# One 256-column broadcast product for the MLP norm factors in place of two of 128 columns, with both diagonals written by one VectorE operation

## Chip, cores and metric

The kernel runs on one core of a Trainium2 chip. The metric is the device time of one execution in microseconds (us), lower is better. TensorE (PE) does the matrix products, VectorE (DVE), ScalarE (ACT) and GpSimd (POOL) the elementwise work, and SyncE (SP) issues the transfers of the weights from HBM. PEld stands for PE's loading of the stationary operand.

## What is computed

The reference is a decoder trunk of two layers, A and B, on 256 tokens of width 1024 in float32. Each layer is an attention part followed by an MLP with a squared ReLU behind an RMS norm. The change touches only the norm of the two MLPs:

```python
def _rmsnorm(x, g):
    xf = x.astype(jnp.float32)
    y = xf * lax.rsqrt(jnp.mean(xf * xf, axis=-1, keepdims=True) + EPS)
    return (y * g.astype(jnp.float32)).astype(x.dtype)

def _sq_relu_mlp(h, w_up, w_down):
    u = jax.nn.relu(h @ w_up)
    return (u * u) @ w_down
...
x = x + _sq_relu_mlp(_rmsnorm(x, a_norm_mlp[i]), a_w_up[i], a_w_down[i])
```

The factor rsqrt(mean + EPS) is one number for each token. The kernel multiplies x by the gains first, runs the up projection on that, and applies the factor of each token to the product, together with the ReLU. This is allowed since the factor is positive and common to a token's row.

## The kernel before

Activations lie transposed: 128 of the 1024 features on the partitions, the 256 tokens along the free dimension, eight such tiles (`xT`). Every float32 weight is split into a high part `wh`, written by ACT (line 336), and a low part `wl`, written by DVE (line 338). A product is then three matmuls: high by high, low by high, high by low.

**The up projection** (`mlp_up`, line 772) runs over 16 blocks, numbered 0 to 15 here. A block is two chunks of weights, each 128 of the 4096 hidden features, and fills one PSUM bank (128 x 512 float32, class `acc`, four banks) with 48 matmuls of 256 columns (line 819). DVE then empties the bank (line 788): ReLU and the multiplication by `rb`, the factors of the 256 tokens spread over all partitions. Block 0's line 788 is the first reader of `rb`.

**The factors.** ACT squares the tiles of x into buffers of the class `sq` (two of them), POOL adds them up (line 450), a small product with a matrix of ones sums over the partitions (line 458), and a chain of short DVE operations (lines 464 to 466) makes the factor `rstd`, 128 partitions x 2: partition p, column h is token 128h + p. **`bcast`** (line 470) turns that into `rb`: for each half h it writes a diagonal matrix, the identity times the factor column (line 475, buffers of the class `dg`), and multiplies it with the matrix of ones on PE (line 477), which leaves the 128 factors of that half in every partition of PSUM. DVE then copies the 256 columns to `rb` (line 479). This happens once in each layer, while PE is in the middle of the up projection.

**What sets the order.** Nothing runs in the order in which it is written. Each operation is given to a planner (`Plan.add`, lines 75 to 116) with its engine, an assumed duration in ns, and the buffers that it reads and writes. `Plan.order` (line 118) simulates the engines, starts whatever is ready with the lowest priority number, and hands out the buffers of a class as they come free, the lowest free number first. A buffer counts as free 200 ns (`LAT`) after the planned end of its last user. The program is then emitted in the planned order, and on the chip each engine works through its own queue in that order and waits on semaphores. So an assumed duration that changes can move instructions on any engine and can hand a buffer to another user. The planner's numbers for `bcast` before are 196 ns for each diagonal and 213 ns for each product.

Of the kernel before, what the change touches and what calls it, by code (L numbers as in the profile page):

```python
# [14 lines left out]
OP = mybir.AluOpType  # L15
AX = mybir.AxisListType

D, S, FF = 1024, 256, 4096
# [194 lines left out]
def t_dve(n, scalar=False):  # L213
    return 69 + 1.041 * n + (61 if scalar else 0)
# [11 lines left out]
def tile_hybrid(ctx: ExitStack, tc: tile.TileContext, xa, xb, memt, xnat, mnat, w0, wall, consts, fgain, out):  # L226
    nc = tc.nc
# [9 lines left out]
    P = Plan(caps, ("acc", "w", "wh", "wl", "v") + tuple(f"B{i}" for i in range(8)))  # L237
    uid = [0]

    def name(s):  # L240
        uid[0] += 1
        return f"{s}_{uid[0]}"

    def buf(cls, shape, dt=F32, pool=None):
        pool = pool or ring
        return Buf(cls, lambda slot: pool.tile(shape, dt, name=name(cls), tag=f"{cls}{slot}", bufs=1))

    def bank(cls):
        return buf(cls, [128, 512], F32, psum)
# [8 lines left out]
    def fixed(shape, nm, dt=F32):  # L258
        return const.tile(shape, dt, name=name(nm))
# [28 lines left out]
    ones = fixed([128, 128], "ones")  # L288
# [5 lines left out]
    ident = fixed([128, 128], "ident")  # L294
# [175 lines left out]
    def bcast(st):  # L470

        ps = bank("t")
        for h in range(2):
            dg = buf("dg", [128, 128])
            P.add(("dve", 196, lambda dg=dg, h=h: nc.vector.tensor_scalar_mul(dg.t, ident, st.r[:, h:h + 1])),
                  [st.key], [dg])
            P.add(("pe", 213, lambda dg=dg, h=h: nc.tensor.matmul(
                ps.t[:, h * 128:(h + 1) * 128], ones, dg.t, start=True, stop=True)), [dg], [ps])
        P.add(("dve", t_dve(S), lambda: nc.vector.tensor_copy(rb_t, ps.t[:, 0:S])), [ps], ["rb"])


# [290 lines left out]
    def mlp_up(st, sums=()):  # L772
# [5 lines left out]
        for b in range(16):  # L778
            u = buf("u", [128, 2, S])
            ps = bank("acc")  # L780
            for mi in range(2):
                wh, wl = chunk()
                up_chunk(ps, mi, wh, wl)
            if first:
                bcast(st)
                first = False
            k0 = 2 * b % 4
            P.add(("dve", t_dve(512, True), lambda u=u, ps=ps: nc.vector.scalar_tensor_tensor(  # L788
                u.t, ps.t.rearrange("p (a s) -> p a s", a=2), 0.0, rb_t[:, None, :].to_broadcast([128, 2, S]),
                op0=OP.max, op1=OP.mult)), [ps, "rb"], [u])  # L790
            P.add(("act", t_act(512), lambda u=u: nc.scalar.activation(u.t, u.t, AF.Square)), [u], [u])  # L791
            if b in sums:
                dst, keys = sums[b]

                def blocks(u=u, dst=dst):
                    a = [u.t[:, k, hf * 128:hf * 128 + 128] for hf in range(2) for k in range(2)]
                    s = [dst()[:, i * 128:i * 128 + 128] for i in range(4)]
                    nc.vector.tensor_add(s[0], a[2], a[3])
                    nc.vector.tensor_sub(s[1], s[0], a[0])
                    nc.vector.tensor_sub(s[2], a[0], a[2])  # L800
                    nc.vector.tensor_sub(s[3], a[1], s[1])
                P.add(("dve", 4 * t_dve(128) + 100, blocks), [u], keys, port=True)
            P.add(("act", t_act(512), lambda u=u, t=us[b // 2], k0=k0: nc.scalar.copy(t.t[:, k0:k0 + 2, 0], u.t)),
                  [u], [(us[b // 2], b)])
            P.add(("dve", t_dve(512), lambda u=u, t=us[b // 2], k0=k0: nc.vector.tensor_sub(
                t.t[:, k0:k0 + 2, 1], u.t, t.t[:, k0:k0 + 2, 0].bitcast(F32))), [u, (us[b // 2], b)],
                [(us[b // 2], b, 1)], port=True)
# [595 lines left out]
```

## Time and profile before

| | |
|---|---|
| median of 3 runs | 595.46 us (594.59 to 595.98) |
| the profiled execution | 598.83 us, of which the span from the first to the last instruction is 597.1 us |
| mean granted TensorE clock | 0.996 |
| busy: PEld / DVE / ACT / POOL | 517.7 / 485.2 / 390.1 / 56.1 us of the span |
| instructions on PE / DVE | 3794 / 869 |
| read from HBM | 106.72 MB, 181 GB/s over the span |

A share of busy time is a mean over the whole span. What a change in one place is worth is read from that place: which engine is working without a pause there, and which wait ends last. In a group's row the columns are the source line, the engine and operation, output<-input with the shape, the count, the busy time and the mean duration of one in ns, and after the second bar the idle time of the engine before these instructions and what ended it. In a timeline row they are the start, the time from the first start to the last end, the engine, the line, the names and the count. Durations include a tail that the next instruction overlaps, so the distance from start to start is shorter than the duration.

### The profile page before, as it was taken

Reading aid. Unit: us, or ns where it says so; the run is one execution under the profiler, and the core shown is the slowest. Engines: PE = TensorE matmul, PEld = TensorE weight load, DVE = VectorE, ACT = ScalarE, POOL = GpSimd, SP = SyncE. Lnnn points to the kernel's source line nnn. Section 1 sums busy time; section 2 is a strip of 40 time slices with the busy share of each in tenths; the row PEclk is TensorE's granted clock in tenths of the full one; section 3 lists DMA queues with packets and bytes.
Section 4 is the critical chain, followed back from the end, with each engine's and each line's share of the span. In section 5 each row is a group of like instructions: output and inputs, shape, how many; then the busy total and the mean of one; then the engine's idle time right before and its main releaser. Section 6 shows DMA issues by size and latency. Waiting matters only on the chain.

```text
span 597.1 us, 10365 instructions
## 1 busy us (share of the span) xinstructions
PE 586.0 (98%) x3794; PEld 517.7 (87%) x3794; DVE 485.2 (81%) x869; ACT 390.1 (65%) x749; POOL 56.1 (9%) x67
## 2 busy tenths in 40 slices
PE   8999999999999999999999999999999999999995
PEld 7777878999999988888888887889999999888884
DVE  6699886789877898988988688786886767998874
ACT  6788797666665575555786588776575565665632
POOL 0131020240000000000122131001300000000002
PEclk9999999999999999999999999999999999999998
DMA  8974715336656536567576633334565555356531
GB/s 302 343 259 137 257 65 167 118 122 228 207 182 209 181 111 224 193 209 247 173 232 233 211 125 124 106 93 159 183 205 199 188 178 177 141 177 245 180 104 71
DMA packets 30003, 108.45 MB, mean 182 GB/s; under 512 B 3328, under 2 KB 3328, under 8 KB 29696
## 3 DMA queue, kind: packets, MB, share of 16 engines
q1 hardware_dynamic: 29664, 107.26, 53.5%
q8 instruction: 30, 0.49, 0.3%
q10 hardware_dynamic: 288, 0.52, 0.2%
q14 instruction: 21, 0.17, 0.1%
HBM read 106.72 MB, written 1.05 MB: 181 GB/s over the span
## 4 chain that ended last, share of the span: by engine, by line
PE 88%; DMA 4%; DVE 4%; ACT 3%; issue 1%; SPq 0%; DVEq 0%; ACTq 0%
PE acc L819 30%; PE t L869 22%; PE acc L497 16%; PE acc L763 7%; PE acc L869 6%; DMA w<-wall 2%; PE t L584 2%; PE t L622 2%; PE t L679 1%; DVE wl L338 1%; DMA w<-memt 1%; ACT wh L336 1%; PE t L555 1%; DMA xT<-xa 1%; DVE xT L749 0%
## 5 line engine op out<-in xcount | busy, mean ns | idle before, releaser
L336 ACT CAST wh<-w 128x512 fp32r<-128x512 f32 (+1 forms) x232 | 182.4, 816 | 119.8 <-PE acc L819 44.5
L338 DVE TENSOR_TENSOR wl<-w,wh 128x512 fp32r<-128x512 f32 (+1 forms) x232 | 213.8, 943 | 32.6 <-ACT wh L336 32.0
L819 PE MATMUL acc<-xn,wh 128*128 128x256 f32 x1024 | 130.2, 279 | 1.1 <-DVE xn L354 1.1
L819 PEld LDWEIGHTS acc<-xn,wh 128*128 128x128 f32 x1024 | 123.4, 188 | 1.5 <-DVE xn L354 1.3
L869 PE MATMUL t<-wh,B 128*128 128x512 f32 (+1 forms) x368 | 111.9, 386 | 0.0
L497 PE MATMUL acc<-wh,xn 128*128 128x512 f32 x256 | 86.1, 404 | 0.9 <-ACT xn L352 0.9
L869 PEld LDWEIGHTS t<-wh,B 128*128 128x128 f32 x368 | 68.5, 188 | 13.8
L869 PE MATMUL t<-wl,B 128*128 128x512 f32 (+1 forms) x184 | 71.0, 386 | 0.0
L819 PE MATMUL acc<-xn,wl 128*128 128x256 f32 x512 | 70.1, 279 | 0.0
L819 PEld LDWEIGHTS acc<-xn,wl 128*128 128x128 f32 x512 | 64.0, 188 | 0.0
L497 PEld LDWEIGHTS acc<-wh,xn 128*128 128x128 f32 x256 | 48.9, 191 | 13.4 <-issue 1.4
L497 PE MATMUL acc<-wl,xn 128*128 128x512 f32 x128 | 50.9, 397 | 0.2 <-DVE wl L338 0.2
L763 PE MATMUL acc<-B,wh 128*128 128x256 f32 x256 | 50.8, 289 | 0.0
L450 POOL TENSOR_TENSOR sqa<-sqa,sq 128x256 f32<-128x256 f32 x21 | 20.3, 966 | 235.4 <-ACT sq L449 234.4
L788 DVE SCALAR_TENSOR_TENSOR u<-acc,rb 128x512 f32<-128x512 f32 x32 | 21.9, 690 | 24.6 <-PE acc L819 24.5
L763 PEld LDWEIGHTS acc<-B,wh 128*128 128x128 f32 x256 | 41.1, 191 | 0.6 <-issue 0.5
L869 PEld LDWEIGHTS t<-wl,B 128*128 128x128 f32 x184 | 34.6, 188 | 7.0
L763 PE MATMUL acc<-B,wl 128*128 128x256 f32 x128 | 36.1, 282 | 0.0
L531 POOL TENSOR_TENSOR ropet<-ropes,consts 128x256 f32<-128x256 f32 (+1 forms) x28 | 25.8, 940 | 105.1 <-ACT ropes L520 77.0
L892 ACT CAST wh<-wsum 128x1024 fp32r<-128x1024 f32 x24 | 25.3, 1052 | 8.6 <-PE acc L819 3.2
L791 ACT ACTIVATE u<-u 128x512 f32<-128x512 f32 x32 | 20.1, 632 | 16.3 <-DVE u L788 16.2
L603 ACT ACTIVATE B<-t,nm 128x128 f32<-128x128 f32 (+1 forms) x64 | 27.1, 440 | 4.6 <-DVE nm L599 2.7
(221 smaller groups left out, 853.7 us busy)
## 6 DMA issues: line engine op xcount, KB each, us to landing
w<-wall SPq DMA_DIRECT2D x191, 512.0 KB, 3.5
w<-memt SPq DMA_DIRECT2D x4, 512.0 KB, 5.1
B<-xnat SPq DMA_DIRECT2D x1, 1024.0 KB, 7.5
B<-mnat SPq DMA_DIRECT2D x1, 1024.0 KB, 9.6
xT<-xa SPq DMA_DIRECT2D x1, 540.0 KB, 4.0
w<-w SPq DMA_DIRECT2D x2, 256.0 KB, 3.5
xT<-xb SPq DMA_DIRECT2D x1, 512.0 KB, 6.8
consts<-consts SPq DMA_DIRECT2D x1, 256.5 KB, 5.1
```

What stands on the lines that cost most here:

```text
L336: P.add(("act", t_act(n), lambda sl=sl: nc.scalar.copy(h.t[:, sl], w.t[:, sl])), [(w, x) for x in q], [(h, x) for x in q])
L338: P.add(("dve", t_dve(n), lambda sl=sl: nc.vector.tensor_sub(l.t[:, sl], w.t[:, sl], h.t[:, sl].bitcast(F32))), [(w, x) for x in q] + [(h, ...
L450: P.add(("pool", t_pool(S), lambda: nc.gpsimd.tensor_tensor(self.acc.t, self.acc.t, sq.t, op=OP.add)), [sq, self.acc], [self.acc])
L497: nc.tensor.matmul(pss[hf].t[:, c0:c1], a(k)[:, ts], b.t[:, o + c0:o + c1], start=(k == 0 and i == 0), stop=(k == KT - 1 and i == 2))
L531: nc.gpsimd.tensor_tensor(t.t[:, 0:nh, e:e + 32], zs.t[:, 0:nh, 32 - e:64 - e], b(sin[:, e:e + 32]), op=OP.mult)
L603: nc.scalar.activation(p[hd].t[:, c], sp[hd].t[:, c], AF.Exp, bias=nm[hd][:, qb:qb + 1], accum_out=ss[:, hd, qb:qb + 1])
L763: nc.tensor.matmul(o, a.t[:, ws], x(k), start=(n == 0 and m % 2 == 0 and i == 0), stop=(n == KT - 1 and i == 2), skip_group_check=True)
L788: P.add(("dve", t_dve(512, True), lambda u=u, ps=ps: nc.vector.scalar_tensor_tensor(u.t, ps.t.rearrange("p (a s) -> p a s", a=2), 0.0, rb_ ...
L791: P.add(("act", t_act(512), lambda u=u: nc.scalar.activation(u.t, u.t, AF.Square)), [u], [u])
L819: nc.tensor.matmul(ps.t[:, o], w.t[:, k * 128:(k + 1) * 128], xnt[:, k, x], skip_group_check=True, **flags)
L869: nc.tensor.matmul(ps.t[:, c0:c1], x, y, start=start and i == 0, stop=stop and i == 2, skip_group_check=True)
L892: P.add(("act", t_act(m), lambda: nc.scalar.copy(h[x].t[:, :m], src())), keys, [h[x]])
```

## The change

```diff
     def bcast(st):
 
         ps = bank("t")
-        for h in range(2):
-            dg = buf("dg", [128, 128])
-            P.add(("dve", 196, lambda dg=dg, h=h: nc.vector.tensor_scalar_mul(dg.t, ident, st.r[:, h:h + 1])),
-                  [st.key], [dg])
-            P.add(("pe", 213, lambda dg=dg, h=h: nc.tensor.matmul(
-                ps.t[:, h * 128:(h + 1) * 128], ones, dg.t, start=True, stop=True)), [dg], [ps])
+        dg = buf("sq", [128, S])
+        P.add(("dve", t_dve(S), lambda: nc.vector.tensor_tensor(
+            dg.t.rearrange("p (a s) -> p a s", a=2), ident[:, None, :].to_broadcast([128, 2, 128]),
+            st.r[:, :, None].to_broadcast([128, 2, 128]), op=OP.mult)), [st.key], [dg])
+        P.add(("pe", 427, lambda: nc.tensor.matmul(ps.t[:, 0:S], ones, dg.t, start=True, stop=True)), [dg], [ps])
         P.add(("dve", t_dve(S), lambda: nc.vector.tensor_copy(rb_t, ps.t[:, 0:S])), [ps], ["rb"])
```

Both diagonals are written by one DVE operation, 128 x 256, whose two inputs are the identity repeated twice and the two factor columns each repeated 128 times. They go to one buffer of the class `sq`, and one product of 256 columns takes the place of the two of 128. The planner now counts 336 ns (`t_dve(256)`) where it counted twice 196, and 427 ns where it counted twice 213. Behind the function every line number is lower by one (819 becomes 818, 788 becomes 787).

The queues of ACT, POOL and SP keep their order. Three places differ.

**DVE in layer B, at the broadcast.** `rstd` is the factor, `sq` the buffer of both diagonals, `rb` the spread factors, `acc` the PSUM banks of up-projection blocks. Before:

```order
L338 TENSOR_TENSOR wl_5029<-w_4864,wh_4976 128x1024 [waits DMAHW4_49,PE_49,Activation_49]
L475 TENSOR_SCALAR dg_5041<-ident_122,rstd_184 128x128
L475 TENSOR_SCALAR dg_5043<-ident_122,rstd_184 128x128
L338 TENSOR_TENSOR wl_5051<-w_4945,wh_5023 128x1024 [waits DMAHW5_49,PE_49,Activation_49]
L479 COPY rb_70<-t_5053 128x256 [waits PE_49]
L338 TENSOR_TENSOR wl_5067<-w_4968,wh_5039 128x1024 [waits DMAHW6_49,Activation_49]
L788 SCALAR_TENSOR_TENSOR u_5081<-acc_4811,rb_70 128x512 [waits DVE_49]
L788 SCALAR_TENSOR_TENSOR u_5091<-acc_4842,rb_70 128x512
```

Now:

```order
L338 TENSOR_TENSOR wl_5026<-w_4861,wh_4973 128x1024 [waits DMAHW4_49,PE_49,Activation_49]
L474 TENSOR_TENSOR sq_5038<-ident_122,rstd_184 128x256 [waits Pool_49]
L338 TENSOR_TENSOR wl_5046<-w_4942,wh_5020 128x1024 [waits DMAHW5_49,PE_49,Activation_49]
L478 COPY rb_70<-t_5048 128x256 [waits PE_49]
L338 TENSOR_TENSOR wl_5061<-w_4965,wh_5036 128x1024 [waits DMAHW6_49,Activation_49]
L787 SCALAR_TENSOR_TENSOR u_5075<-acc_4808,rb_70 128x512 [waits DVE_49]
L787 SCALAR_TENSOR_TENSOR u_5085<-acc_4839,rb_70 128x512
```

Two operations became one, at the same place in the queue, and it now waits for POOL, whose adding-up was the last reader of that `sq` buffer. Layer A's DVE queue changes in the same way.

**PE in layer A, at the broadcast.** `acc_1625` is the bank of block 2, `t_1813` the broadcast product. Before:

```order
L819 MATMUL acc_1625<-xn_67,wh_1568 128x256 x2
L819 MATMUL acc_1625<-xn_67,wl_1635 128x256 x8
L477 MATMUL t_1813<-dg_1805,ones_116 128x128 [waits DVE_49,PE_49]
L477 MATMUL t_1813<-dg_1807,ones_116 128x128 [waits DVE_49]
L819 MATMUL acc_1625<-xn_67,wh_1612 128x256 x16
```

Now:

```order
L818 MATMUL acc_1625<-xn_67,wh_1568 128x256 x2
L818 MATMUL acc_1625<-xn_67,wl_1635 128x256 x8
L818 MATMUL acc_1625<-xn_67,wh_1612 128x256 x2
L477 MATMUL t_1813<-sq_1805,ones_116 128x256 [waits DVE_49,PE_49]
L818 MATMUL acc_1625<-xn_67,wh_1612 128x256 x14
```

The broadcast product moved behind two matmuls of block 2.

**PE in layer B, from the broadcast to block 4.** `acc_4871` (now `acc_4868`) is the bank of block 2, `acc_5093` (now `acc_5087`) that of block 3, `acc_5166` (now `acc_5160`) that of block 4. Before:

```order
L819 MATMUL acc_4871<-xn_67,wl_4846 128x256 x8
L477 MATMUL t_5053<-dg_5041,ones_116 128x128 [waits DVE_49,PE_49]
L477 MATMUL t_5053<-dg_5043,ones_116 128x128 [waits DVE_49]
L819 MATMUL acc_4871<-xn_67,wh_4824 128x256 x16
L819 MATMUL acc_4871<-xn_67,wl_4918 128x256 x8
L819 MATMUL acc_5093<-xn_67,wh_4928 128x256 [waits Activation_49]
L819 MATMUL acc_5093<-xn_67,wh_4928 128x256 x15
```

Now:

```order
L818 MATMUL acc_4868<-xn_67,wl_4843 128x256 x8
L477 MATMUL t_5048<-sq_5038,ones_116 128x256 [waits DVE_49,PE_49]
L818 MATMUL acc_4868<-xn_67,wh_4821 128x256 x16
L818 MATMUL acc_4868<-xn_67,wl_4915 128x256 x8
L818 MATMUL acc_5087<-xn_67,wh_4925 128x256 [waits DVE_49,Activation_49]
L818 MATMUL acc_5087<-xn_67,wh_4925 128x256 x15
```

The places are the same, but block 3's first matmul now waits for DVE as well. The planner hands block 3 the bank of block 0, which line 787 empties just before, where it handed it the fourth bank before: the planned end of that DVE operation came 55 ns earlier, which puts the release of block 0's bank ahead of block 3's planned start and no longer behind it. From there on, blocks 4 to 15 alternate between the same two banks as before, in the other phase. In layer A no bank changes.

## The prediction

> **What bounds the kernel now.** I read the page's first part, then busy time in stretches of 100 us, then who made PE wait, and last the timeline around the two broadcasts.
>
> ```profile
> PE 586.0 (98%) x3794; PEld 517.7 (87%) x3794; DVE 485.2 (81%) x869; ACT 390.1 (65%) x749; POOL 56.1 (9%) x67
> 100.00:200.00 100.00, 98.91 (x862) 98.17 (x861) 80.83 (x150) 64.79 (x115) 10.46 (x11) 1.00 0.53 174
> 400.00:500.00 100.00, 100.00 (x850) 99.39 (x850) 75.33 (x123) 58.99 (x84) 7.10 (x7) 1.00 0.57 189
> PE acc L819 <- DVE xn L354: 1.1, 1, 1.1
> ```
>
> In the two stretches with a broadcast in them (layer A near 140 us, layer B near 430 us) PE is busy for 98.9 and 100.0 of 100 us (the numbers behind the comma are PE, PEld, DVE, ACT and POOL, then the granted clock, 1.00). The longest PE wait of the up projections is 1.1 us, once, for a tile of x. So the end is set by PE's own queue: an edit counts in full if it makes PE's work there longer or shorter, or makes PE wait, and not at all if it moves DVE within the cover that PE's work gives it. An execution would have to move by 1.2 us (0.2% of 595.46) to be told from no change.
>
> What is edited is small. The groups of the two lines:
>
> ```profile
> L477 PE MATMUL t<-dg,ones 128*128 128x128 f32 x8 | 1.2, 273 | 0.0
> L475 DVE TENSOR_SCALAR dg<-ident,rstd 128x128 f32<-128x128 f32 x4 | 1.0, 280 | 0.0
> ```
>
> All of it is 1.2 us of PE and 1.0 us of DVE in both layers together. Even if the change made both free, PE would gain about 1 us. The trace has eight matmuls for four products: each float32 product is two instructions.
>
> The timeline in layer B, which carries the terms:
>
> ```profile
> 429.06 0.48 DVE L475 TENSOR_SCALAR dg<-ident,rstd 128x128 f32<-128x128 f32 x2
> 429.25 0.28 DVE L475 TENSOR_SCALAR dg<-ident,rstd 128x128 f32<-128x128 f32 x1
> 429.45 1.22 DVE L338 TENSOR_TENSOR wl<-w,wh 128x1024 fp32r<-128x1024 f32 x1
> 429.94 0.52 PEld L477 LDWEIGHTS t<-dg,ones 128*128 128x128 f32 x4
> 430.06 0.60 PE L477 MATMUL t<-dg,ones 128*128 128x128 f32 x4
> 430.39 1.95 PEld L819 LDWEIGHTS acc<-xn,wh 128*128 128x128 f32 x16
> 430.70 0.42 DVE L479 COPY rb<-t 128x256 f32<-128x256 f32 x1
> 431.04 1.22 DVE L338 TENSOR_TENSOR wl<-w,wh 128x1024 fp32r<-128x1024 f32 x1
> 432.17 0.68 DVE L788 SCALAR_TENSOR_TENSOR u<-acc,rb 128x512 f32<-128x512 f32 x1
> 433.21 1.96 PEld L819 LDWEIGHTS acc<-xn,wh 128*128 128x128 f32 x16
> ```
>
> and in layer A:
>
> ```profile
> 139.40 0.47 DVE L475 TENSOR_SCALAR dg<-ident,rstd 128x128 f32<-128x128 f32 x2
> 139.79 1.22 DVE L338 TENSOR_TENSOR wl<-w,wh 128x1024 fp32r<-128x1024 f32 x1
> 140.14 0.53 PEld L477 LDWEIGHTS t<-dg,ones 128*128 128x128 f32 x4
> 140.59 1.90 PEld L819 LDWEIGHTS acc<-xn,wh 128*128 128x128 f32 x16
> 140.93 0.42 DVE L479 COPY rb<-t 128x256 f32<-128x256 f32 x1
> ```
>
> **Term 1, PE's own work.** Removed at each broadcast: four matmuls of 128 columns with their weight loads, which hold PE's queue from 429.94 to 430.39 (140.14 to 140.59 in A), 0.45 us, 0.1125 each. Added: two matmuls of 256 columns. The columns streamed are the same, so the first guess is twice 2 x 0.1125 = 0.45 us, a difference of 0. Float32 matmuls of that width stand elsewhere:
>
> ```profile
> 86.55 1.08 PE L679 MATMUL t<-ppx,mv 128*64 128x256 f32 x8
> 87.56 1.09 PE L622 MATMUL t<-ident,B 128*128 128x128 f32 x8
> L679 PE MATMUL t<-B,vb 128*64 128x256 f32 x24 | 3.9, 400 | 0.0
> ```
>
> Eight of them in 87.56 - 86.55 = 1.01 us are 0.126 each, but with half the array's columns each, two heads writing side by side; if pairs run at the same time, one takes 0.25. The low end is thus 2 x 0.126 = 0.25 us, a gain of 0.20 at each broadcast and 0.40 in all. The high end is two that do not overlap at all, by the mean duration of the last row 2 x 0.40 = 0.80, a loss of 0.35 each and 0.70 in all. I take 0: the rows of this very product, scaled by columns, are the nearest.
>
> **Term 2, DVE's operation and PE's wait for it.** The two diagonals take 429.45 - 429.06 = 0.39 us of the queue. The nearest rows for the new operation:
>
> ```profile
> L537 DVE TENSOR_TENSOR B<-ropes,consts 128x256 f32<-128x256 f32 x4 | 1.7, 420 | 1.0 <-ACT ropes L520 1.0
> L354 DVE SCALAR_TENSOR_TENSOR xn<-xT,xn x32: 476/480/962, 5.7 to 418.8; 128x256 fp32r<-128x256 f32 x32
> 419.79 4.16 POOL L450 TENSOR_TENSOR sqa<-sqa,sq 128x256 f32<-128x256 f32 x3 [0.35 <-ACT sq L449]
> 128.58 5.93 POOL L450 TENSOR_TENSOR sqa<-sqa,sq 128x256 f32<-128x256 f32 x5 [2.06 <-ACT sq L449]
> ```
>
> L537 is a tensor_tensor of 256 columns with one input repeated: 0.42 us long, as L479 is, and L479 holds the queue for 431.04 - 430.70 = 0.34. So I take 0.34, that is 0.05 less than the two diagonals. The high end is the slowest 256-column operation with two inputs that the trace has, 0.96 in L354, twice its median. I don't expect that doubling: L354 makes its tiles while POOL adds up their squares, and at the diagonals POOL has been idle for 5 us (its rows end at 423.95 and 134.51). The low end is a single diagonal's 0.28.
>
> [...]
>
> PE's turn at the product comes at 429.94, and the last diagonal ends at 429.06 + 0.48 = 429.54, 0.40 earlier. With 0.42 long, the new one ends at 429.48; with 0.96, at 430.02, and PE would wait for about 0.1. In A the old pair ends at 139.87, 0.27 ahead of PE's turn at 140.14, and the product now stands two matmuls later: 1.90/16 = 0.12 each, 0.24 more cover. So PE waits 0 at both places. The new wait for POOL in front of the operation is for work that was over 5 us before: 0. What is queued behind it on DVE is L338 and then the copy to `rb`.
>
> **Term 3, the new wait of block 3 in layer B.** Its first weights are loaded at 433.21, and it now needs the bank that the first L788 reads until 432.17 + 0.68 = 432.85. A release costs about 0.04 (the broadcast product ends at 430.06 + 0.60 = 430.66, the copy that waits for it starts at 430.70). That leaves 433.21 - 432.89 = 0.32 us of cover, so 0. The chain into L788 is the product, the copy, L338, L788. The product would end where it ended: its second matmul starts at 430.06 + 0.225 and lasts 0.40, so 430.69 against 430.66. DVE itself would be free 0.05 earlier. So L788 moves by less than 0.05 either way. Blocks 4 to 15 reuse a bank that was emptied a whole block earlier (a block lasts some 5.6 us, twice the 2.8 from the weights at 430.39 to those at 433.21): no cover is lost there.
>
> **Term 4, the moved product in layer A.** It starts 0.24 later, so the copy comes near 140.93 + 0.2, and L788 with it. Behind it on DVE stand the low parts of weights; the one that follows the copy directly is used by PE in block 5's first chunk, some two and a half blocks of 5.6 us later: covered, 0. POOL, ACT and SP keep their order. SP's transfers wait for DVE's progress in
>
> ```profile
> SPq L313 <- DVE wl L338: 385.5, 138, 13.2
> ```
>
> and would be issued at most 0.2 later; PE's waits name no transfer, so 0.
>
> **Sum:** 0 + 0 + 0 + 0. The profiled execution of 598.83 us (span 597.1) would repeat itself; it lies 3.4 above the median, and since the forecast is a difference, I put it on the median of 595.46: 595.4.
>
> **Rivals.**
> 1. *The wide product is cheaper than its columns.* For it: the 0.126 of L679, and four weight loads fewer in both layers together. Against it: L679 uses half the array, and PEld is as full as PE around the broadcasts, so it is not clear that loads are what a stream waits for. 0.20 at each broadcast: 595.46 - 0.40 = 595.06.
> 2. *Slower, by the bank of block 3.* If L788 of layer B ends over 0.32 us later than now, PE stands still until it does, and everything behind it on PE with it. It decides from 433.17 on. A slow form of the new operation (0.96 long, some 0.5 more of the queue) brings L788 to about 432.85 + 0.4, hence 0.1 of stall; a copy held up by a product that does not overlap adds 0.35 to both PE and L788. Price 0.1 to 0.8 with term 1's high end: 595.6 to 596.3. For it: the cover is thinner than any other in the up projection. Against it: three rows would have to be wrong together for more than 0.5.
> 3. *The change does not do what it says*, if the product of 256 columns were still issued in pieces of 128. The new order shows one row for each broadcast. Time: 595.46.
>
> **How the numbers follow.** Forecast of no change 0.78, first rival 0.10, second 0.10, third 0.02. None of them reaches 1.2 us by its price; what is left for the outer cases is a wait that I did not see and the scatter of a median, so 0.92 for within 0.2%, 0.04 for faster, 0.04 for slower. The range takes in the ends, 595.46 - 0.40 and 595.46 + 0.8, and beyond them half a microsecond below, since three runs of one kernel spread from 594.59 to 595.98: 594.5 to 596.3.
>
> **What would show it.** Term 1: the product's two weight loads to the next L818 load 0.45 apart. Term 2: the new operation about 0.42 long, 0.34 to the next DVE start, and no PE wait named for it. Term 3: the first L787 over before the weights of block 3, no PE wait for `u`; a PE idle row there would prove rival 2. Term 4: the copy in A some 0.2 later. PE 3790 and DVE 867 instructions if the change does what it says. A difference of over 1.2 us would make the prediction wrong, above all one outside 425 to 440 us and 135 to 150 us, where nothing was edited.

## The result, and the profile after

The changed kernel took 602.69 us (median of 6 runs, 602.08 to 603.36), the kernel before 595.92 (6 runs beside them, 594.59 to 598.80). The ratio is 1.0091 with a 95% interval of 1.0070 to 1.0113: slower by 5.4 us, between 4.2 and 6.7 (the two medians lie 6.8 apart; the kernel before's own runs spread over 4.2). The prediction was no change, 594.5 to 596.3. The profiled execution took 602.71 us with a span of 600.9, where that of before took 598.83 and 597.1.

The page and PE's waits of the changed kernel:

```profile
PE 589.3 (98%) x3790; PEld 520.5 (87%) x3790; DVE 484.5 (81%) x867; ACT 390.3 (65%) x749; POOL 56.1 (9%) x67
PE acc L496 <- ACT wh L336: 1.4, 1, 1.4
PE acc L818 <- DVE xn L354: 1.1, 1, 1.1
```

PE has four instructions fewer, as the change says, and is busy for 3.3 us longer. No wait has come near the broadcasts (the 1.4 us stands at the start of the program). So PE did not wait more; it worked more slowly. Where is seen in the stretches of 25 us that lie wholly in the up projections. The columns are the stretch, its length, the busy time and number of instructions of PE, PEld, DVE, ACT and POOL, the granted clock, DMA's busy share and GB/s. Before:

```profile
150.00:175.00 25.00, 25.00 (x223) 25.00 (x222) 20.21 (x32) 15.12 (x19) 0.00 (x0) 1.00 0.62 205
175.00:200.00 25.00, 25.00 (x223) 25.00 (x223) 18.55 (x27) 15.27 (x19) 0.00 (x0) 1.00 0.58 195
450.00:475.00 25.00, 25.00 (x214) 25.00 (x214) 18.30 (x27) 14.69 (x19) 0.00 (x0) 1.00 0.55 189
475.00:500.00 25.00, 25.00 (x215) 25.00 (x214) 19.30 (x30) 13.71 (x18) 0.00 (x0) 1.00 0.58 188
```

After:

```profile
150.00:175.00 25.00, 25.00 (x215) 25.00 (x214) 19.02 (x29) 15.21 (x20) 0.00 (x0) 1.00 0.57 190
175.00:200.00 25.00, 25.00 (x215) 25.00 (x214) 18.74 (x30) 14.08 (x18) 0.00 (x0) 1.00 0.55 190
450.00:475.00 25.00, 25.00 (x214) 25.00 (x214) 18.24 (x27) 14.70 (x19) 0.00 (x0) 1.00 0.56 192
475.00:500.00 25.00, 25.00 (x214) 25.00 (x213) 17.93 (x27) 14.09 (x17) 0.00 (x0) 1.00 0.54 185
```

In layer A (the first two rows) PE did 223 matmuls in 25 us before and 215 after, with the same matmul, the same clock of 1.00 and no pause in either. In layer B the profiled execution of before already stood at 214 and 215. So there are two paces, and the profile of before has one in each layer. The timeline gives them exactly. Before in A, before in B, after in A (a row is 16 matmuls by a high part; the 8 by a low part stand between the rows):

```profile
143.43 1.98 PE L819 MATMUL acc<-xn,wh 128*128 128x256 f32 x16
...
154.31 1.98 PE L819 MATMUL acc<-xn,wh 128*128 128x256 f32 x16
```

```profile
433.33 2.05 PE L819 MATMUL acc<-xn,wh 128*128 128x256 f32 x16
...
444.63 2.05 PE L819 MATMUL acc<-xn,wh 128*128 128x256 f32 x16
```

```profile
144.58 2.05 PE L818 MATMUL acc<-xn,wh 128*128 128x256 f32 x16
...
155.89 2.05 PE L818 MATMUL acc<-xn,wh 128*128 128x256 f32 x16
```

Between each pair lie 96 matmuls: 10.88/96 = 113.3 ns from one to the next, 11.30/96 = 117.7, 11.31/96 = 117.8. I call these the quick and the slow beat. Start by start, the quick beat repeats 113, 113, 114 ns and the slow one 119, 117, 118, 118 and the like, and either was kept to the end of the stage: behind the broadcast all steps but the first lie between 113 and 116 ns in A before, and between 117 and 119 in B before and in both layers after. Behind the broadcast come 648 matmuls in each layer: 648 x 4.5 ns = 2.9 us for a layer in the slow beat.

This accounts for the two profiled executions. From the first up-projection matmul behind the broadcast to the first down-projection matmul layer A took from 140.62 to 214.15 before, 73.5 us, and from 141.80 to 218.07 after, 76.3. That is 2.7 of the 3.8 us between the spans (two matmuls fewer are in it, since the broadcast moved behind them). Another 1.1 was there before the first up projection began, where the starts of these executions differ. Layer B was slow in both. At the quick beat the profiled execution of before would have taken an estimated 598.83 - 2.9 = 595.9 us, where the median of the kernel's runs lies.

The 14 profiles of this case (the two here and the twelve below) settle what else can differ. Take from each span the start, up to the first up-projection matmul, and both up projections, from first to last matmul: what is left is 289.9 to 290.1 us in all of them. The start took 124.13 to 126.93 us. An up projection without added matmuls took 89.6 to 90.4 us with the quick beat behind the broadcast and 92.4 to 93.1 with the slow one. So nothing but the start and the beats made the profiled times of such kernels differ. By these figures, an execution of the kernel before that took 595.98 us and was slow in layer B would have come to its first up projection at 595.98 - 1.77 - 289.95 - 89.59 - 93.09 = 121.6 us, 2.5 earlier than in any profile (1.77 is by how much the profiled time of before, 598.83, exceeds its span). So unless they started that early, layer B was quick in the four fastest of the six runs of before, 594.59 to 595.98. This estimate makes the loss some 2.8 us in each layer, 5.6 in both, which lies within the measured 4.2 to 6.7.

### The profile page after: what moved, and what is told of

Read it like the earlier page. It is cut to its first block, busy times and chain, and to the rows that moved or that the text cites. A ratio compares the mean times of both kernels' runs of the same rounds, so it can differ in the third digit from the quotient of the medians.

```text
span 600.9 us, 10356 instructions
## 1 busy us (share of the span) xinstructions
PE 589.3 (98%) x3790; PEld 520.5 (87%) x3790; DVE 484.5 (81%) x867; ACT 390.3 (65%) x749; POOL 56.1 (9%) x67
## 4 chain that ended last, share of the span: by engine, by line
PE 88%; DVE 4%; DMA 4%; ACT 3%; issue 1%; SPq 0%; DVEq 0%; ACTq 0%
PE acc L818 30%; PE t L868 22%; PE acc L496 15%; PE acc L762 7%; PE acc L868 6%; PE t L583 2%; PE t L621 2%; DVE wl L338 1%; PE t L678 1%; DMA B<-xnat 1%; PE t L554 1%; ACT wh L336 1%; DMA w<-memt 1%; DMA w<-w 1%; ACT B L432 1%
## 5 line engine op out<-in xcount | busy, mean ns | idle before, releaser
L818 PE MATMUL acc<-xn,wh 128*128 128x256 f32 x1024 | 132.4, 282 | 1.1 <-DVE xn L354 1.1
L818 PEld LDWEIGHTS acc<-xn,wh 128*128 128x128 f32 x1024 | 125.4, 189 | 1.7 <-DVE xn L354 1.3
L818 PE MATMUL acc<-xn,wl 128*128 128x256 f32 x512 | 71.1, 281 | 0.0
L818 PEld LDWEIGHTS acc<-xn,wl 128*128 128x128 f32 x512 | 64.9, 189 | 0.0
L787 DVE SCALAR_TENSOR_TENSOR u<-acc,rb 128x512 f32<-128x512 f32 x32 | 21.9, 690 | 27.5 <-PE acc L818 27.5
```

The source lines that it names most:

```text
L818: nc.tensor.matmul(ps.t[:, o], w.t[:, k * 128:(k + 1) * 128], xnt[:, k, x], skip_group_check=True, **flags)
```

## Experiments

Twelve further runs were made, the last of the kernel before itself. For each its time, its ratio to the kernel before with the interval, and the beat behind the place in question, read from its profile as above (in the rest of the text "quick" and "slow" are the beats; a stretch of 25 us with 222 or 223 matmuls is quick, one with 214 or 215 slow).

**e1: the changed kernel with two products of 128 columns again.**

```diff
-        P.add(("pe", 427, lambda: nc.tensor.matmul(ps.t[:, 0:S], ones, dg.t, start=True, stop=True)), [dg], [ps])
+        def product():
+            for h in range(2):
+                nc.tensor.matmul(ps.t[:, h * 128:(h + 1) * 128], ones, dg.t[:, h * 128:(h + 1) * 128],
+                                 start=True, stop=True)
+        P.add(("pe", 427, product), [dg], [ps])
```

> The changed kernel with its one DVE operation, its buffer, its order and its banks, but the product again in two of 128 columns from that buffer. Theory (beat): in the profiles the 646 to 648 up-projection matmuls behind a broadcast start 113.3 or 117.8 ns apart, for a whole stage; the four-instruction product of before changes the beat that the sums' product left behind, the two-instruction product keeps it. Then layer A runs at 113.3 behind the broadcast and the time goes back by 2.9 us in A, and in B as often as before: about 596 to 599. Rival (the DVE operation, the moved product or the bank of block 3): nothing of that is undone here, so 602 to 603, with 117.8 in both layers.

598.80 us (595.61 to 600.72), ratio 0.9999 (0.9972 to 1.0026). One stretch of each layer:

```profile
150.00:175.00 25.00, 25.00 (x223) 25.00 (x222) 20.21 (x32) 14.82 (x19) 0.00 (x0) 1.00 0.58 206
450.00:475.00 25.00, 25.00 (x223) 25.00 (x222) 19.61 (x32) 15.28 (x19) 0.00 (x0) 1.00 0.57 191
```

Both layers are quick, and the loss is gone, with the one DVE operation, the moved place in A and the other bank of block 3 all kept. So these three cost nothing that could be measured here. The profiled execution, 595.61, is the fastest of the ten; the beats of the other nine are not known.

**e2: the changed kernel with two DVE operations for the diagonals.**

```diff
-        P.add(("dve", t_dve(S), lambda: nc.vector.tensor_tensor(
...
+        def diagonals():
+            for h in range(2):
+                nc.vector.tensor_scalar_mul(dg.t[:, h * 128:(h + 1) * 128], ident, st.r[:, h:h + 1])
+        P.add(("dve", t_dve(S), diagonals), [st.key], [dg])
```

> The changed kernel with its one product of 256 columns, but the two diagonals written by two DVE operations as before, into the halves of the one buffer. Theory (beat): the product is what counts, so 117.8 ns behind the broadcast in both layers and 602 to 603. Rival (the DVE operation): about 596 to 599.

602.15 us (601.47 to 604.11), ratio 1.0082 (1.0053 to 1.0111), slow in both layers. With e1 this shows what of the change costs: the loss comes and goes with the shape of the product. Layer B of this execution adds a case. The quick beat came into the product here:

```profile
430.58 1.07 PE L819 MATMUL acc<-xn,wl 128*128 128x256 f32 x8
431.49 0.62 PE L819 MATMUL acc<-xn,wh 128*128 128x256 f32 x4
431.94 1.07 PE L819 MATMUL acc<-xn,wl 128*128 128x256 f32 x8
432.85 0.59 PE L478 MATMUL t<-sq,ones 128*128 128x256 f32 x2
433.09 2.23 PE L819 MATMUL acc<-xn,wh 128*128 128x256 f32 x16
435.16 1.10 PE L819 MATMUL acc<-xn,wl 128*128 128x256 f32 x8
436.10 2.05 PE L819 MATMUL acc<-xn,wh 128*128 128x256 f32 x16
437.99 0.28 PE L819 MATMUL acc<-xn,wl 128*128 128x256 f32 x1
```

Eight matmuls take 431.49 - 430.58 = 0.91 us ahead of the product, 114 ns each, and 436.10 - 435.16 = 0.94 behind it, 118 each. So the wide product did not merely keep the beat that it met, as I had put it in the expectation of e1: it left the slow beat from both.

**e3 and e4: two further one-column products (four instructions) directly behind the broadcast,** in the changed kernel and in the kernel before. Their results are not read. In e3:

```diff
+            for h in range(2):
+                nc.tensor.matmul(ps.t[:, S + h:S + h + 1], dg.t[:, h * 128:(h + 1) * 128], ones[:, 0:1],
+                                 start=True, stop=True)
```

> The changed kernel with two further float32 products of one column (four instructions, about 0.36 us of PE by the rows of line 458) right behind the 256-column product, into columns of PSUM that nobody reads. Theory (beat): four short instructions change the beat, as line 458 does, so from 117.8 to 113.3 in A; 602.7 + 0.7 - 2.9 to 602.7 + 0.7 - 5.8: 597.5 to 600.5, faster although work was added. Rival (the wide product costs, or DVE, bank or order): 602.7 + 0.7 = 603.4.

602.94 us (602.00 to 603.83), ratio 1.0078 (1.0050 to 1.0106), slow in both layers: the theory's number missed. The group of four short instructions at once behind the wide product did not bring the quick beat: 214 or 215 matmuls in 25 us in both layers.

> The kernel before with the same two further one-column products behind its second 128-column product. Theory (beat): one more change of the beat, so A goes from 113.3 to 117.8 behind the broadcast: 595.9 + 0.7 + 2.9 to 595.9 + 0.7 + 5.8: 599.5 to 602.4, for 0.7 us of work. Rival (work alone): 596.6.

602.43 us (601.53 to 602.98), ratio 1.0068 (1.0041 to 1.0095). Layer A was slow behind the group, as expected, with the quick beat ahead of it; layer B was quick, with the slow beat ahead of it. The time, at the upper end of what was expected for two slow layers, does not show layer B's quick beat: the profiled execution, 601.53, is the fastest of the four and came to its first up projection 1.5 us later than that of before (125.99 against 124.45); the beats of the other three are not known.

**e5 and e6: further float32 products of 128 columns in the changed kernel, but later,** between blocks 4 and 5 of each up projection, ones by ones into a bank that nobody reads, two of them (four instructions) in e5 and one in e6:

```diff
+            if b == 4:
+                fl = bank("t")
+
+                def flip(fl=fl):
+                    for i in range(2):
+                        nc.tensor.matmul(fl.t[:, i * 128:(i + 1) * 128], ones, ones, start=True, stop=True)
+                P.add(("pe", 2 * 213, flip), ["rb"], [fl])
```

> The changed kernel with two further float32 products of 128 columns (ones by ones, four instructions, 0.45 us of PE in each layer by the rows of line 477 of before) put in between blocks 4 and 5 of each up projection, into a bank that nobody reads. In the runs so far a group of four 128-column instructions that met the 117.8 ns beat left 113.3 behind it each time. Theory (beat): 117.8 from the broadcast to these products, 113.3 from there to the end of the up projection, 528 matmuls x 4.5 ns = 2.4 us less in each layer: 602.7 + 0.9 - 4.8 = 598.8, faster for more work. Rival (something else of the change costs, the beat goes with it): 603.6.

599.19 us (597.34 to 600.86), ratio 1.0024 (1.0005 to 1.0044). That is 3.5 us less than the changed kernel's 602.69 although 0.9 us of work was added, 0.4 above the number expected. It is also 3.2 less than e6 below, which ran beside it and has half the added work at the same place. Layer A of its profile:

```profile
153.39 2.05 PE L825 MATMUL acc<-xn,wh 128*128 128x256 f32 x16
155.27 1.11 PE L825 MATMUL acc<-xn,wl 128*128 128x256 f32 x8
156.22 0.61 PE L791 MATMUL t<-ones 128*128 128x128 f32 x4
156.58 2.08 PE L825 MATMUL acc<-xn,wh 128*128 128x256 f32 x16
158.50 1.07 PE L825 MATMUL acc<-xn,wl 128*128 128x256 f32 x8
159.40 1.98 PE L825 MATMUL acc<-xn,wh 128*128 128x256 f32 x16
161.22 0.96 PE L825 MATMUL acc<-xn,wl 128*128 128x256 f32 x7
```

16 matmuls take 155.27 - 153.39 = 1.88 us ahead of the four and 161.22 - 159.40 = 1.82 behind them, 117.5 and 113.8 ns each. Layer B turned in the same way. This is the plainest evidence that the beat is what costs: nothing of the change was undone.

> The same with one product of 128 columns there, two instructions. If the number of columns of an instruction is what counts, the beat changes as with four: 602.7 + 0.45 - 4.8 = 598.3. If the number of instructions counts, 117.8 stays: 603.2.

602.44 us (602.04 to 604.64), ratio 1.0088 (1.0056 to 1.0121), slow throughout in both layers:

```profile
165.00:190.00 25.00, 25.00 (x214) 25.00 (x214) 18.75 (x31) 14.43 (x18) 0.00 (x0) 1.00 0.55 184
460.00:485.00 25.00, 25.00 (x214) 25.00 (x214) 17.63 (x26) 14.09 (x17) 0.00 (x0) 1.00 0.55 186
```

Two instructions did not turn the beat here even at 128 columns, with 214 matmuls in 25 us behind them. So it was not that 256 columns keep it and 128 break it.

**e7: the kernel before with one further 256-column product behind the sums of line 458,** so that the slow beat should always come into the broadcast:

```diff
+                if wide:
+                    nc.tensor.matmul(ps.t[:, S:2 * S], ones, self.acc.t, start=True, stop=True)
```

> The kernel before with one further float32 product of 256 columns behind each layer's two sums (line 458), in the middle of the up projection and ahead of the broadcast, into columns of PSUM that nobody reads; 0.43 us of PE each. A product of 256 columns left 117.8 behind it in all cases so far, whichever beat it met, and the broadcast's four 128-column instructions then made 113.3 of it in all four cases. Theory (beat): 113.3 behind the broadcast in both layers in every run, while the kernel before has it in layer B only in some: the lowest times of before plus 0.9, 596 to 597, with none of its higher times. Rival (a beat of chance): a spread as wide as before's, 596 to 600.

598.60 us (596.13 to 598.96), ratio 1.0016 (0.9997 to 1.0034). The profile has the quick beat behind the broadcast in both layers, as expected, but the times do not lie where I put them, and the spread is not settled by the beat alone: the runs spread over 2.8 us, as much as the starts of the 14 profiles do (124.13 to 126.93). No gain can be claimed for this kernel.

**e8 to e11: other groups at the place of e5,** again from the slow beat: two products of 256 columns (e8), three and four of 128 (e9, e10), two of 64 (e11), all with `rb` as the second operand and nobody reading the result.

> The changed kernel with two float32 products of 256 columns between blocks 4 and 5 of each up projection (four instructions of 256 columns, 0.86 us of PE each time, into a bank that nobody reads). What is asked is the beat of the 528 up-projection matmuls behind them, when 117.8 ns come in. If four instructions are what changes the beat: 113.3 behind them in both layers, 602.7 + 1.7 - 4.8 = 599.6. If the columns of an instruction are (128 change it, 256 keep it): 117.8, 604.4.

603.89 us, ratio 1.0112 (1.0078 to 1.0146): slow in both layers.

> The same with three products of 128 columns (six instructions, 0.68 us). If three short instructions or more change the beat: 113.3, 602.7 + 1.4 - 4.8 = 599.3. If each pair counts as one turn and only an even number of turns reaches the other beat: 117.8, 604.1.

603.25 us, ratio 1.0084 (1.0057 to 1.0112): slow in both.

> The same with four products of 128 columns (eight instructions, 0.90 us). If a group of four flips the beat once, eight flip it back: 117.8, 604.5. If a long enough group of short instructions always ends the 117.8 beat: 113.3, 602.7 + 1.8 - 4.8 = 599.7.

599.31 us, ratio 1.0015 (0.9989 to 1.0041): quick in both. Twice the added work of e5, at the same time:

```profile
165.00:190.00 25.00, 25.00 (x223) 25.00 (x222) 18.70 (x28) 14.20 (x18) 0.00 (x0) 1.00 0.58 195
460.00:485.00 25.00, 25.00 (x223) 25.00 (x222) 19.01 (x27) 14.92 (x19) 0.00 (x0) 1.00 0.58 198
```

> The same with two products of 64 columns (four instructions, about 0.45 us if the weight loads set their pace). If the number of instructions counts: 113.3, 602.7 + 0.9 - 4.8 = 598.8. If each must last as long as one of 128 columns: 117.8, 603.6.

600.73 us, ratio 1.0061 (1.0027 to 1.0095): quick in A, slow in B.

**e12: the kernel before once more,** for a second profile.

> The kernel before, unchanged, for a second profile of it. Theory (beat): behind the broadcast of layer A 113.3 again. In layer B it depends on the beat that comes into the sums' product: if 113.3 comes in, the sums leave 117.8, the broadcast leaves 113.3, and 2.9 us of the first profile's 598.83 are gone (about 596); if 117.8 comes in, it ends with 117.8, near 598.8. Rival (layer B of the kernel before always runs at 117.8): 117.8 behind the broadcast in B, whatever comes in.

597.54 us, ratio 1.0004 (0.9972 to 1.0036). Quick in both layers:

```profile
150.00:175.00 25.00, 25.00 (x223) 25.00 (x222) 20.13 (x30) 16.23 (x22) 0.00 (x0) 1.00 0.58 195
450.00:475.00 25.00, 25.00 (x223) 25.00 (x222) 18.43 (x27) 14.44 (x18) 0.00 (x0) 1.00 0.59 199
```

So layer B of the kernel before can run quick, and the rival falls. The path to it was not the one that I had written: the slow beat came into the sums' product and was still there behind it, and the broadcast turned it.

What a group of float32 matmuls left behind, by what came in, over the profiles (the broadcasts of e3 and e4 and the sums of e7 are left out, since other float32 matmuls follow them at once):

| group | slow beat in | quick beat in |
|---|---|---|
| 2 of 256 columns, the changed broadcast | slow, 15 of 15 | slow, 1 of 1 |
| 4 of 256 (e8) | slow, 2 of 2 | |
| 2 of 128 (e6) | slow, 2 of 2 | |
| 4 of 128, the broadcast before, e1, e7, e12; and e5 | quick, 9 of 9 | slow, 1 of 1 |
| 6 of 128 (e9) | slow, 2 of 2 | |
| 8 of 128 (e10) | quick, 2 of 2 | |
| 4 of 64 (e11) | quick 1, slow 1 | |
| 4 of one column (the sums of line 458) | quick 3, slow 6 | slow, 17 of 17 |

No group had the quick beat behind it when the quick beat came in. From the slow beat, the sums' four one-column instructions left now the one and now the other. This is also why layer B of the first profile of before was slow: its sums had turned the slow beat into the quick one, and the broadcast's four instructions met that.

## Why the prediction was wrong

**The step that failed** is the sum's silent one: "an edit counts in full if it makes PE's work there longer or shorter, or makes PE wait, and not at all if it moves DVE within the cover". I priced what the product itself holds of PE's queue and took the pace of the 648 matmuls behind it as given: term 1, "PE's own work", has nothing for it. That pace changed. The two instructions of the wide product left the slow beat of 117.8 ns, 2.9 us in each layer, where the four of the two products left the quick one of 113.3 in A in every profile (before, e1, e7, e12) and in B in all of these but the first of before. None of the three rivals had it. The bound that I drew from the groups ("even if the change made both free, PE would gain about 1 us") holds for the product alone. The high end of 596.3 was added up from the product's own length and a stall of block 3, and lies 6.4 us short of the measured median. The sign of being wrong that the prediction names did come: the loss of layer A lies between 141.80 and 218.07 us, for the most part outside the stretch of the edit.

**The sign of it stood in the rows that I quoted.** The weight loads of 16 matmuls were "1.90" at 140.59 and "1.95" and "1.96" at 430.39 and 433.21, the same instructions in the same program, and I read from them only that PE had no pause. The profiled execution's 3.4 us above the median was another sign, and I passed over it. PE was 100% busy at both paces, with 223 and with 214 or 215 matmuls in 25 us.

**Term 1** was right about the product itself. In A the broadcast starts at 141.56 and the eight low-part matmuls behind the next 14 at 143.64: 2.08 less 14 x 0.1178 is 0.43 us, where I took 0.45. The sign that I had named, from its first weight load to the next load of L818, was 0.33 in layer B (434.19 - 433.86 in the rows below) and not 0.45. The 16 loads behind it took 436.17 - 434.19 = 1.98, 0.10 more than 16 x 0.1178, which makes up the rest.

**Term 2** was right. The changed kernel's DVE and PEld rows in layer B, with A's copy as the first:

```profile
142.19 0.42 DVE L478 COPY rb<-t 128x256 f32<-128x256 f32 x1 [0.18 <-PE t L477]
...
432.87 0.42 DVE L474 TENSOR_TENSOR sq<-ident,rstd 128x256 f32<-128x256 f32 x1
433.20 1.22 DVE L338 TENSOR_TENSOR wl<-w,wh 128x1024 fp32r<-128x1024 f32 x1
434.60 0.42 DVE L478 COPY rb<-t 128x256 f32<-128x256 f32 x1 [0.18 <-PE t L477]
434.94 1.22 DVE L338 TENSOR_TENSOR wl<-w,wh 128x1024 fp32r<-128x1024 f32 x1
436.08 1.28 DVE L787 SCALAR_TENSOR_TENSOR u<-acc,rb 128x512 f32<-128x512 f32 x2
```

```profile
433.86 0.31 PEld L477 LDWEIGHTS t<-sq,ones 128*128 128x128 f32 x2
434.19 2.05 PEld L818 LDWEIGHTS acc<-xn,wh 128*128 128x128 f32 x16
436.17 1.02 PEld L818 LDWEIGHTS acc<-xn,wl 128*128 128x128 f32 x8
437.11 1.01 PEld L818 LDWEIGHTS acc<-xn,wh 128*128 128x128 f32 x8
```

The operation is 0.42 long and holds the queue for 433.20 - 432.87 = 0.33 us; I took 0.42 and 0.34. PE did not wait for it.

**Term 3** was right in its answer. A single L787 was 0.68 long before, so the first is over near 436.08 + 0.68 = 436.76, and block 3's weights are loaded at 437.11: 0.35 us, less the 0.04 of a release 0.31, where I had 0.32. The copy waited 0.18 us for the product, since DVE was free earlier than I had counted. It cost nothing: from the product's first weight load to the first L787 it is 436.08 - 433.86 = 2.22 us, where it was 432.17 - 429.94 = 2.23 to L788 before, within the 0.05 that I had allowed.

**Term 4** was right: from the start of the diagonals' operation to the copy A took 1.53 us before (139.40 to 140.93) and 1.73 after (140.46 to 142.19), 0.2 later. Only the copy itself waited, 0.18 us for the product, and PE did not.

## What to carry to other kernels

Where PE is 100% busy with one kind of matmul for many microseconds, count its instructions in equal stretches: two counts for the same matmul at the same clock were two paces here (223 and 214 in 25 us, at 1.00), and a small edit in the middle of such a stream can change which of them the whole rest of the stage has, as one product did here (73.5 us against 76.3 behind it in layer A). Price an edit in such a stream by the instructions behind it times the difference of the paces (648 x 4.5 ns = 2.9 us here), not by its own length alone. Look at the paces in several profiles of the kernel before, since one profile shows only one draw: layer B of the kernel before had 214 and 215 matmuls in 25 us in the first and 223 in that of e12.

## What the runs showed of the hardware

A stream of float32r matmuls of 256 columns, each with its own weight load of 128 columns, kept one of two beats, 113.3 or 117.8 ns, at a granted clock of 1.00 in both. What came behind a group of ordinary float32 matmuls went with the group. When the slow beat came in, 2 or 6 of 128 columns left the slow beat (2 of 2 each) and 4 or 8 the quick one (9 of 9 and 2 of 2); one wide pair left the slow one from either (15 of 15 and 1 of 1). No run shows the mechanism. Why 4 and 8 turned it and 2 and 6 did not, and why 4 of 64 columns did both, stays open.

The start of the program moved too. The first up projection began at 124.13 us in the profile of e1 and at 126.93 in that of e11. This is why e12's profiled execution, quick in both layers, took 598.33 us, only 0.5 less than the first one of before with its slow layer B: it came to the first up projection 2.2 us later (126.64 against 124.45). In the profiles of kernels without added matmuls, start and beats are all of the spread but 0.2 us. The beats of the executions without a profile are only inferred, and what moves the start is open. No version was found that beats the kernel before.
